# Output projection in block products: a pool per weight tile, later accumulating loads, and all gate sums in one stage

## The chip, the core and the metric

The kernel runs on one core of one Trainium2 chip. The metric is the device time of one execution in microseconds, the median over the runs shown. TensorE (PE) multiplies, VectorE (DVE) and ScalarE (ACT) work on elements, GpSimd (POOL) and SyncE (SP) here mostly issue DMA transfers, each engine from a queue of its own in order.

## The reference

One block of a network over 512 tokens of width 2048, float32 throughout:

```python
sh_a, sc_a, g_a, sh_f, sc_f, g_f = split(silu(c) @ ada_w + ada_b, 6)
h = rms_norm(x, norm_mix) * (1 + sc_a) + sh_a
proj = h @ w_in                       # 2048 x 5656
y_conv = group_norm(short_conv(...))  # 1024 columns, 8 groups of 128
y_attn = head_norm(sparse_attention(...))  # 1024 columns, 8 heads of 128
x = x + g_a * (concat([y_conv, y_attn]) @ w_out)         # 2048 x 2048
h = rms_norm(x, norm_ffn) * (1 + sc_f) + sh_f
x = x + g_f * ((silu(h @ ffn_w1) * (h @ ffn_w3)) @ ffn_w2)   # 2048 x 5632, 5632 x 2048
```

The change touches three places of it: the six conditioning rows (a vector of 2048 times ada_w, 2048 x 12288), the product with w_out, and the place in time at which the row g_f is formed.

## The kernel before

**Arithmetic.** Every large float32 product is three matmuls: each operand is split into a rounded high part and the rest, and high x low, low x high and high x high are added up in PSUM. For a weight tile of 128 x 1024 ACT casts the high part (`whi`) and DVE subtracts it for the low part (`wlo`). Both go to rings of three buffers, so DVE can be about two tiles ahead of PE. An engine runs its queue in order: a DVE instruction that waits for a DMA holds back every `wlo` behind it.

**Stages.** The first fill, norm and the key, value and query columns (to about 320 us); the convolution's columns in eight groups (`conv(c)`), with the attention steps woven in (to 681 us); the output projection (681 to 878); the first projection of the FFN, 44 column blocks (878 to 1749); the second projection (1749 to the end). Within a stage the source gives the order of the work; the framework sets the order of each engine's queue from it by its own planned times, so a transfer or instruction whose wait it expects to end later can fall behind one that stands later in the source. `tc.issue_after(i)` puts what is in its block behind instruction `i` on `i`'s engine.

**Conditioning rows.** They are summed on DVE: for each of 16 slices a piece of ada_w is loaded and added with its factor. `ada(...)` does so with 512 or 1024 columns at once; `gates_beside()` runs steps of it beside the convolutions, at the rates given to `beside`. The gate g_a goes to the DRAM rows `gad[0..3]`. The row g_f (2048 columns in four blocks of 512, 16 sums each) is made by `gate_sums()` (L1739), a generator: each step loads one piece on POOL's queue into `accs` (L1745) and then adds it with the next step (L1748). One buffer holds the piece, so the next load waits for the sum. `next(sums)` stands in the loop of the first projection (every 8th product) and in that of the second (every 3rd unit, L2045).

**Output projection.** The product of the 512 x 2048 input y and w_out is cut into 2 x 2 blocks on both sides, and a Strassen scheme with seven products is used instead of eight: product p (named 2, 1, 5, 6, 3, 7, 4 in this order) multiplies a sum of blocks of y by a sum of blocks of w_out. Each product has eight units (p, j), one for each 128 rows of the weights; a unit is 12 matmuls of 512 columns (4 output tiles x 3 parts, `y_mm`, L1209). The order of the 56 units:

```python
def y_units():
    yield from ((p, j) for p in (2, 1, 5) for j in range(HK))
    for j in range(0, HK, 2):
        yield from ((6, j), (6, j + 1), (3, j), (3, j + 1)) if j in (0, HK - 2) else ((6, j), (3, j), (6, j + 1), (3, j + 1))
    yield from ((p, j) for p in (7, 4) for j in range(HK))
```

`y_load(p, j)` loads the weights of a unit, `y_split` (L1197, L1199) makes `whi` and `wlo` two units ahead, `y_form` (L1040, L1041) splits y's part. The weights of products 1, 5, 6 and 4 share one tile `WT[j]` of a pool `wt` with eight buffers: 1 loads it (L1171), 5 adds another block by an accumulating DMA on POOL (L1173), 6 adds a third on DVE from product 3's tile (L1407), 4 adds a fourth by DMA (L1182). Product 7 loads a tile and accumulates onto it by DMA (L1176 to L1180). The `wt` pool lies where the masks, the attention's keys, values and queries (`qkv`) were, so its loads wait until those are no longer read. The products' sums go through PSUM to `x2T` and others, with x loaded by `x_load` (L1293, L1302) on SP, squared for the next norm, and stored by `x_store` (L1309) on POOL. `at_unit(p, j, ...)` names work ahead of a unit, `behind_unit` work behind it; `yat` gives a unit's number.

The convolution's output is normed late: `norm_y` sums the squares on PE, takes the root on ACT and DVE (L147), stores the row and loads it back to all partitions (L246, L1093, both on POOL), and `scale_y` multiplies (L1100). For the last group this falls into the output projection, and the last sums of y's blocks (`y_sum`, L1028 to L1033) and forms wait for it:

```python
    for n in range(-5, 4):
        if yu[n + 5][0] == 2:
            y_load(*yu[n + 5])
        if n + 2 >= 0:
            y_split(*yu[n + 2])
        if n >= 0:
            y_multiply(*yu[n])

    norm_y()
```

**Second projection.** Again seven products over blocks, in four groups: 154 units of 12 matmuls (L1943; the first unit L1933), with `w_load`, `w_split` (L1529, L1915) and accumulating loads on POOL (L1894, L1899, L1903).

Of the kernel before, what the change touches and what calls it, by code (L numbers as in the profile page):

```python
# [10 lines left out]
F32 = mybir.dt.float32  # L11
F32R = mybir.dt.float32r
# [58 lines left out]
def block_kernel(ctx: ExitStack, tc: tile.TileContext, a: dict, out: bass.AP):  # L71
# [487 lines left out]
    qT = [qp.tile([P, R, S], F32, name=f"qT{g}") for g in range(NKV)]  # L559
# [547 lines left out]
    class Places:  # L1107
# [3 lines left out]
        def tile(self, shape, dtype, tag, name):  # L1111
            self.n += 1
            if shape[1] == 512:
                return kT[self.n % 2][self.n // 2 % 2]
            free = [kTt[:, 0].rearrange("p g s -> p (g s)"), kTt[:, 1].rearrange("p g s -> p (g s)"),
                    yct[:, 6:8, :].rearrange("p c s -> p (c s)")]
            return free[self.n % (3 if self.convs_out < 5 else 2)]
# [3 lines left out]
    def gates_beside():  # L1121
        yield from ffn_part(places, 512, 2)
# [7 lines left out]
        for j in (2, 0):  # L1130
            got = []
            yield from ada(places, 1024, 2 * D + j * 512, 1024, got, bias=True)
            for t in range(2):
                half = got[0][:, t * 512:(t + 1) * 512]
                nc.scalar.activation(half[:, :P], quarters(half), AF.Copy, scale=1.0 if j else -1.0)
                row_of(gad[j + t], half)
            yield
            yield

    later = gates_beside()  # L1140
    weave(beside(convs(), later, (0.3,) * 24 + (0.62,)), attention_steps(), 0.59 / 3)
# [22 lines left out]
    def y_load(p, j):  # L1164
# [3 lines left out]
        elif p == 1:  # L1168
            for q in (1, 5, 6, 4):
                WB[q, j] = in_four(WT[j])  # L1170
            nc.sync.dma_start(WB[p, j], w_block(1, 1, j))  # L1171
        elif p == 5:
# [13 lines left out]
    def y_split(p, j):  # L1186
# [3 lines left out]
        else:  # L1190
            hi, lo = [[wtp.tile([P, 1024], F32R, tag="wt", name="w4")] for _ in range(2)] if p == 4 and j > 4 else \
# [41 lines left out]
    for n in range(-5, 4):  # L1233
        if yu[n + 5][0] == 2:
            y_load(*yu[n + 5])
        if n + 2 >= 0:
            y_split(*yu[n + 2])
        if n >= 0:
            y_multiply(*yu[n])

    norm_y()
# [5 lines left out]
    scale_y()  # L1247
# [17 lines left out]
    wtp = pool("wt", HK, stack=gst)  # L1265
    WT = [wtp.tile([P, 1024], F32, tag="wt", name="wt") for j in range(HK)]
# [22 lines left out]
    def x_load(r, c):  # L1289
        for t in range(2):  # L1290
            if (r, c) == (2, 2):
                for n in range(2):
                    nc.sync.dma_start(x2_of(r, c, t, n),  # L1293
                                      x_of(r, c, t)[:, n * 512:(n + 1) * 512].rearrange("p (a b) -> p a b", a=2))
                continue
# [6 lines left out]
            nc.sync.dma_start(to, x_of(r, c, t).rearrange("p (a b) -> p a b", a=4))  # L1302

# [95 lines left out]

    def at_unit(p, j, *todo):  # L1400
        steps_at.setdefault(yat[p, j], []).extend(todo)

    for j in range(HK):
        at_unit(*yu[4 + j // 2], (y_load, 1, j))
        at_unit(*yu[7 + j], (y_load, 5, j))
# [684 lines left out]
```

## Time and profile before

| | |
|---|---|
| median of 3 runs | 2223.15 us (2222.48 to 2228.21) |
| profiled execution | 2226.84 us, span 2225.1 us |
| granted clock of PE | 0.988 over the span |
| HBM traffic | 428.19 MB read, 19.96 MB written |

A row of groups names line, engine, operation and output <- input. "SPq" and "POOLq" are issues on a DMA queue. A row of waits reads: engine, tile and line, what ended the wait, then total us, how often, and the longest. A row of a timeline: start, duration, engine, line, operation, count, and in brackets the idle time just before it with what ended it. A row of windows: the stretch, its length, then busy us (and count) of PE, PEld (weight load), DVE, ACT and POOL, the granted PE clock, the DMA engines' share and GB/s; for a query of one line the instructions of that line alone. Busy times of pipelined matmuls overlap, so work is better counted in matmuls than in busy time.

### The profile page before, as it was taken

The page shows a single profiled execution, that of the slowest core. Times are in us where ns is not written, and L with a number is a line of the kernel's source. Part 1 is how long each engine was busy: PE and PEld are TensorE (multiplying, and loading weights), DVE is VectorE, ACT ScalarE, POOL GpSimd, SP SyncE. Part 2 cuts the span into 40 slices and gives each one's busy share as a digit, 9 for nine tenths or more (in the row PEclk, how much of TensorE's full clock was granted, in tenths as well). Part 3 has the DMA queues.
Part 4 walks back from the last instruction along what each step waited for, and adds up shares of the span by engine and source line. Part 5 has one row for each costly group of instructions (what it writes and reads, how often), then busy time and mean ns, then how long its engine had stood idle before and what let it go on. Part 6 is the DMA issues. An engine that isn't in the chain of part 4 may idle for free. (4 is left out here: it accounts for less than half of the span.)

```text
span 2225.1 us, 30860 instructions
## 1 busy us (share of the span) xinstructions
PE 2142.4 (96%) x11453; PEld 1789.9 (80%) x11453; DVE 1763.8 (79%) x2574; ACT 1044.1 (47%) x1663; POOL 255.6 (11%) x327
## 2 busy tenths in 40 slices
PE   7999999999998999999999999999999899997999
PEld 6778788887886778888888888888888777886787
DVE  7789568887886776888888878888888677877688
ACT  4235245554454547544444444444444444443343
POOL 0000200000001120001111110111110222212110
PEclk9999999999999999999999999999999999999999
DMA  9976546665665893597777777788685889896775
GB/s 339 364 242 200 181 148 190 190 214 176 211 196 188 220 250 100 147 238 191 191 184 193 188 187 171 186 191 196 176 194 114 281 219 257 231 239 155 241 169 143
DMA packets 449351, 450.19 MB, mean 202 GB/s; under 512 B 20386, under 2 KB 378826, under 8 KB 448560
## 3 DMA queue, kind: packets, MB, share of 16 engines
q1 hardware_dynamic: 376508, 330.90, 47.8%
q0 software_dynamic: 72160, 116.83, 26.4%
q8 instruction: 90, 1.47, 0.3%
q14 instruction: 61, 0.50, 0.1%
q10 hardware_dynamic: 532, 0.48, 0.1%
HBM read 428.19 MB, written 19.96 MB: 201 GB/s over the span
## 5 line engine op out<-in xcount | busy, mean ns | idle before, releaser
L1529 ACT CAST whi<-raw 128x1024 fp32r<-128x1024 f32 x246 | 258.0, 1051 | 260.3 <-PE main L1542 121.9
L1542 PE MATMUL main<-hC,whi 128*128 128x512 f32 x1408 | 346.0, 392 | 1.3 <-DVE d L1561 1.1
L1536 DVE TENSOR_TENSOR wlo<-raw,whi 128x1024 fp32r<-128x1024 f32 x218 | 265.9, 1220 | 100.2 <-PE aux L1548 49.8
L1529 ACT CAST whi<-t 128x1024 fp32r<-128x1024 f32 x186 | 195.4, 1051 | 263.0 <-PE main L1943 69.3
L1542 PEld LDWEIGHTS main<-hC,whi 128*128 128x128 f32 x1408 | 257.4, 188 | 52.6 <-DVE d L1561 2.6
L1542 PE MATMUL aux<-hC,whi 128*128 128x512 f32 x1072 | 264.1, 391 | 0.0
L1542 PEld LDWEIGHTS aux<-hC,whi 128*128 128x128 f32 x1072 | 196.4, 188 | 38.2 <-issue 0.4
L1548 PE MATMUL main<-hC,wlo 128*128 128x256 f32 x1408 | 191.0, 283 | 0.0
L1548 PEld LDWEIGHTS main<-hC,wlo 128*128 128x128 f32 x1408 | 184.8, 191 | 7.7
L121 PE MATMUL main<-alo,whi 128*128 128x512 f32 x432 | 174.6, 404 | 0.0
L122 PE MATMUL main<-ahi,wlo 128*128 128x512 f32 x432 | 170.1, 394 | 0.0
L123 PE MATMUL main<-ahi,whi 128*128 128x512 f32 x432 | 169.9, 394 | 0.0
L1943 PE MATMUL aux<-wlo,ghi 128*128 128x512 f32 x308 | 124.5, 405 | 25.5 <-DVE wlo L1915 25.4
L1548 PE MATMUL aux<-hC,wlo 128*128 128x256 f32 x1072 | 147.6, 283 | 0.0
L1548 PEld LDWEIGHTS aux<-hC,wlo 128*128 128x128 f32 x1072 | 141.7, 191 | 6.1
L1915 DVE TENSOR_TENSOR wlo<-t,whi 128x1024 fp32r<-128x1024 f32 x102 | 123.6, 1219 | 20.4 <-ACT whi L1529 20.1
L1536 DVE TENSOR_TENSOR wlo<-t,whi 128x1024 fp32r<-128x1024 f32 x84 | 102.5, 1220 | 44.5 <-PE aux L1548 21.3
L1519 POOL DMA_DIRECT2D t<-in_ffn_w x42 | 65.0, 1547 | 535.7 <-DVE d L1557 201.9
L1943 PE MATMUL aux<-whi,glo 128*128 128x512 f32 x308 | 123.4, 401 | 0.0
L1943 PE MATMUL main<-wlo,ghi 128*128 128x512 f32 x304 | 120.1, 395 | 3.4 <-DVE wlo L1915 2.8
L1943 PE MATMUL aux<-whi,ghi 128*128 128x512 f32 x308 | 122.7, 398 | 0.0
L1943 PE MATMUL main<-whi,glo 128*128 128x512 f32 x304 | 119.5, 393 | 0.0
(424 smaller groups left out, 4229.2 us busy)
## 6 DMA issues: line engine op xcount, KB each, us to landing
raw<-in_ffn_w SPq DMA_DIRECT2D x204, 512.0 KB, 5.3
t<-in_ffn_w POOLq DMA_DIRECT2D x90, 512.0 KB, 7.2
t<-in_ffn_w SPq DMA_DIRECT2D x78, 512.0 KB, 5.5
kT<-in_ada_w SPq DMA_DIRECT2D x65, 512.0 KB, 4.6
araw<-in_ada_w SPq DMA_DIRECT2D x56, 512.0 KB, 8.7
raw<-in_w_in SPq DMA_DIRECT2D x128, 192.0 KB, 3.7
raw<-in_w_in SPq DMA_DIRECT2D x38, 512.0 KB, 6.8
accs<-in_ada_w POOLq DMA_DIRECT2D x64, 256.0 KB, 3.8
```

What stands on the lines that cost most here:

```text
L121: nc.tensor.matmul(ps, lhs[0], rhs[1], start=first, stop=False)
L122: nc.tensor.matmul(ps, lhs[1], rhs[0], start=False, stop=False)
L123: return nc.tensor.matmul(ps, lhs[0], rhs[0], start=False, stop=last).ins
L1519: nc.gpsimd.dma_start(b["t"].rearrange("p (k n) -> p k n", k=HK), block(u, 12), accum_op=ALU.add)
L1529: hi_ins[-1] = nc.scalar.copy(hi, t).ins
L1536: lo_ins[-1] = nc.vector.tensor_sub(lo, t, hi.bitcast(F32)).ins
L1542: nc.tensor.matmul(ps, wt[0][:, k * P:(k + 1) * P], hc(p, k), start=first and k == 0, stop=False, skip_group_check=True)
L1548: nc.tensor.matmul(ps[:, HS:], wt[1][:, k * P:(k + 1) * P], hc(p, k)[:, 0:HS], start=False, stop=last and k == HK - 1, skip_group_check=True)
L1915: W["last"] = nc.vector.tensor_sub(lo, t, hi.bitcast(F32)).ins
L1943: nc.tensor.matmul(ps[2 * t + c], x_[:, j, tok], w[:, cs], start=m == 0 and j == 0 and p in (1, 5, 2), stop=m == 2 and j == GS[b] - 1 and ...
```

## The change

- The pools: each of the eight `WT[j]` is its own pool of one buffer, and each of the two query tiles `qT` has its own.
- Product 2's loop runs two units further before the rest of the preparation; `norm_y` for the last group stands ahead of it, and `scale_y` behind the last split.
- Product 5's first four weight blocks are loaded plainly on SP into the ring and added on DVE (`w_sum`) instead of accumulated by DMA. Product 1's loads start two units later in the source; product 4's accumulating loads move from units 32 to 39 to units 40 to 45; product 3's first four loads come four units later.
- x's block (2, 2) is loaded in four pieces at units 24 to 30 instead of all at unit 24; x's block (1, 1) two units later; forms, stores and some sums move to other units.
- Beside the convolutions the gate parts come in another order: the FFN part goes last, one g_a part of 1024 columns becomes two of 512, more places serve as buffers, and the rates change.
- `gate_sums` runs in the first projection alone, every 4th product instead of every 8th.

```diff
-    qT = [qp.tile([P, R, S], F32, name=f"qT{g}") for g in range(NKV)]
+    qT = [pool(f"queries{g}", 1, stack=qk).tile([P, R, S], F32, name=f"qT{g}") for g in range(NKV)]
...
-                    yct[:, 6:8, :].rearrange("p c s -> p (c s)")]
-            return free[self.n % (3 if self.convs_out < 5 else 2)]
+                    yct[:, 6:8, :].rearrange("p c s -> p (c s)"), yct[:, 4:6, :].rearrange("p c s -> p (c s)")]
+            n = 4 if self.convs_out < 4 else 3
+            assert self.convs_out < 6
+            return free[self.n % n]
...
     def gates_beside():
-        yield from ffn_part(places, 512, 2)
...
-        for j in (2, 0):
+
+        def gate_out(j, half):
+            nc.scalar.activation(half[:, :P], quarters(half), AF.Copy, scale=1.0 if j > 1 else -1.0)
+            row_of(gad[j], half)
+
+        got = []
+        yield from ada(places, 1024, 2 * D + 1024, 1024, got, bias=True)
+        for t in range(2):
+            gate_out(2 + t, got[0][:, t * 512:(t + 1) * 512])
+        yield
+        yield
+        for j in range(2):
             got = []
-            yield from ada(places, 1024, 2 * D + j * 512, 1024, got, bias=True)
-            for t in range(2):
-                half = got[0][:, t * 512:(t + 1) * 512]
-                nc.scalar.activation(half[:, :P], quarters(half), AF.Copy, scale=1.0 if j else -1.0)
-                row_of(gad[j + t], half)
+            yield from ada(places, 512, 2 * D + j * 512, 512, got, bias=True)
+            gate_out(j, got[0])
             yield
-            yield
+        yield from ffn_part(places, 512, 2)
 
     later = gates_beside()
-    weave(beside(convs(), later, (0.3,) * 24 + (0.62,)), attention_steps(), 0.59 / 3)
+    weave(beside(convs(), later, (0.3,) * 24 + (0.56,) * 120 + (1.08,)), attention_steps(), 0.59 / 3)
...
+        elif p == 5 and j < 4:
+            WB["b", j] = ring_place()
+            nc.sync.dma_start(WB["b", j], w_block(1, 2, j))
         elif p == 5:
             nc.gpsimd.dma_start(WB[p, j], w_block(1, 2, j), accum_op=ALU.add)
...
-            hi, lo = [[wtp.tile([P, 1024], F32R, tag="wt", name="w4")] for _ in range(2)] if p == 4 and j > 4 else \
+            hi, lo = [[wtp[2 * j - 10 + h].tile([P, 1024], F32R, tag="wt", name="w4")] for h in range(2)] if p == 4 and j > 4 else \
...
-    for n in range(-5, 4):
-        if yu[n + 5][0] == 2:
+    norm_y()
+    for n in range(-5, 6):
+        if n + 5 < HK:
             y_load(*yu[n + 5])
         if n + 2 >= 0:
             y_split(*yu[n + 2])
         if n >= 0:
             y_multiply(*yu[n])
 
-    norm_y()
     y_places("H3")
     y_sum("H3", 0, 1)
     for f in ("E5", "H6", "H3"):
         y_sum(f, 2)
     y_form(1, 6)
-    scale_y()
+    with tc.issue_after(low_of[-1]):
+        scale_y()
     y_form(1, 7)
...
-    wtp = pool("wt", HK, stack=gst)
-    WT = [wtp.tile([P, 1024], F32, tag="wt", name="wt") for j in range(HK)]
+    wtp = [pool(f"wt{j}", 1, stack=gst) for j in range(HK)]
+    WT = [wtp[j].tile([P, 1024], F32, tag="wt", name="wt") for j in range(HK)]
...
+    def x22_load(t, n):
+        nc.sync.dma_start(x2_of(2, 2, t, n), x_of(2, 2, t)[:, n * 512:(n + 1) * 512].rearrange("p (a b) -> p a b", a=2))
...
+    def w_sum(to, j, one):
+        nc.vector.tensor_add(WB[to, j], WB[to, j], WB[one, j])
+
     for j in range(HK):
-        at_unit(*yu[4 + j // 2], (y_load, 1, j))
-        at_unit(*yu[7 + j], (y_load, 5, j))
-        at_unit(*yu[(9, 10, 11, 12, 17, 19, 25, 26)[j]], (y_load, 3, j))
-        at_unit(*yu[yat[6, j] - 5], (lambda j: nc.vector.tensor_add(WB[6, j], WB[6, j], WB[3, j]), j))
+        at_unit(*yu[6 + j // 4 if j < 7 else 9], (y_load, 1, j))
+        at_unit(*yu[6 + j if j < 4 else 7 + j], (y_load, 5, j))
+        if j < 4:
+            at_unit(*yu[12 + j], (w_sum, 5, j, "b"))
+        at_unit(*yu[(13, 14, 15, 16, 17, 19, 25, 26)[j]], (y_load, 3, j))
+        at_unit(*yu[yat[6, j] - 4], (lambda j: nc.vector.tensor_add(WB[6, j], WB[6, j], WB[3, j]), j))
         at_unit(*yu[(28, 30, 32, 34, 37, 38, 39, 40)[j]], (y_load, 7, j))
-        at_unit(*yu[32 + j], (y_load, 4, j))
+        at_unit(*yu[(40, 41, 41, 42, 43, 44, 44, 45)[j]], (y_load, 4, j))
...
-    at_unit(1, 0, (x_load, 1, 1))
+    at_unit(1, 2, (x_load, 1, 1))
     at_unit(1, 4, (x_load, 1, 2))
-    at_unit(6, 0, (x_load, 2, 2))
+    for q in range(4):
+        at_unit(*yu[24 + 2 * q], (x22_load, q // 2, q % 2))
...
-    for p, after in ((5, 2), (6, 1), (3, 5), (7, 6), (4, 3)):
-        for j in range(HK):
-            behind_unit(after, j, (y_form, p, j))
+    for j in range(HK):
+        for p, n in ((5, 8 + j), (6, 16 + j), (3, max(23, 22 + j)), (7, 30 + j), (4, 38 + j)):
+            behind_unit(*yu[n], (y_form, p, j))
...
-        behind_unit(*((6, 4), (3, 4), (6, 5), (3, 5))[q], (fifth, t, n))
+        behind_unit(*yu[(30, 32, 33, 35)[q]], (fifth, t, n))
...
-        behind_unit(5, 6, (x_store, 1, 1, t))
-        behind_unit(7, 4, (x_store, 1, 2, t))
+        behind_unit(6, 0, (x_store, 1, 1, t))
+        behind_unit(7, 7, (x_store, 1, 2, t))
...
-    for n in range(4, len(yu)):
-        for what, *args in [t for m in range(4 if n == 4 else 0) for t in behind.pop(m, ())] + steps_at.get(n, []):
+    for n in range(6, len(yu)):
+        for what, *args in [t for m in range(6 if n == 6 else 0) for t in behind.pop(m, ())] + steps_at.get(n, []):
...
-                with tc.issue_after(W.get("last") or lo_ins[-1]):
+                with tc.issue_after(lo_ins[-1]):
                     nc.vector.scalar_tensor_tensor(acc, raw, cT[:, k:k + 1], acc, op0=ALU.mult, op1=ALU.add)
...
-        if n >= SINGLE and n % 8 == 0:
+        if n >= SINGLE and n % 4 == 0:
             next(sums, None)
...
-        if n % 3 == 0 and b < 3:
-            next(sums, None)
         loads(n)
```

More of the change, by code (lines that the diff above doesn't have):

```diff
@@ L1290, in x_load @@
         for t in range(2):
[L1291 to L1295, printed above, removed]
             if r == 2:
@@ L1435, in block_kernel @@
     for jj in range(4):
-        behind_unit(1, 2 + jj, (lambda jj: nc.vector.scalar_tensor_tensor(YF["E5"][jj], YF["H6"][jj], -1.0, YF["H7"][jj],
+        behind_unit(5, 2 * jj, (lambda jj: nc.vector.scalar_tensor_tensor(YF["E5"][jj], YF["H6"][jj], -1.0, YF["H7"][jj],
                                                                      op0=ALU.mult, op1=ALU.subtract), jj))
@@ L1735, in block_kernel @@
             late = new[-1]
-    W = {}
     def gate_sums():
@@ L1839, in block_kernel @@
     y2 = [(yq if t == 3 else yp).tile([P, D], F32, tag="y", name="y") for t in range(NT)]
-    A_, bank = {}, {}
+    W, A_, bank = {}, {}, {}
     def a_parts(b, p):
```

## The prediction

> **What bounds the kernel now.** I read the page first, then busy time by stage, then the waits of TensorE (PE), then the timelines around the longest of them.
>
> ```profile
> PE 2142.4 (96%) x11453; PEld 1789.9 (80%) x11453; DVE 1763.8 (79%) x2574; ACT 1044.1 (47%) x1663; POOL 255.6 (11%) x327
> ...
> core 0: us, PE busy (x) PEld busy (x) DVE busy (x) ACT busy (x) POOL busy (x), PEclk, DMA share, GB/s
> 681.30:878.00 196.70, 172.34 (x765) 139.28 (x764) 137.02 (x193) 101.97 (x182) 34.25 (x45) 0.95 0.74 201
> 878.00:1749.30 871.30, 869.97 (x5009) 765.96 (x5008) 721.09 (x966) 425.33 (x596) 92.19 (x90) 1.00 0.75 183
> 1749.30:2221.00 471.70, 436.80 (x1869) 354.01 (x1867) 366.84 (x372) 203.67 (x198) 98.58 (x140) 0.97 0.81 215
> ...
> 2108.78 16.32 PE main L1943 x72
> ```
>
> PE is the bound, but not evenly. The three stretches are the output projection, the first projection of the FFN and its second projection. The last line, from the chain that ended last, gives the undisturbed pace: 72 matmuls of 512 columns in 16.32 us, 0.2267 us each, 2.72 us for a unit of twelve. The second projection has 154 units, 1848 matmuls: 418.9 us at that pace, and it takes 471.7, so 52.8 us are lost. The first projection loses next to nothing (869.97 busy of 871.30). The output projection:
>
> ```profile
> 681.30:878.00 196.70, 162.81 (x672) 127.96 (x672) 0.95 0.74 201
> 681.30:878.00 196.70, 9.98 (x64) 9.49 (x64) 0.95 0.74 201
> 704.00:747.00 43.00, 29.02 (x113) 21.93 (x114) 26.37 (x41) 19.29 (x34) 8.97 (x12) 0.88 0.93 250
> 812.00:835.00 23.00, 17.80 (x69) 13.61 (x67) 11.40 (x17) 7.59 (x13) 5.50 (x7) 0.93 1.08 258
> ```
>
> The first two lines are the products (L1209) and the turning of the result (L1369) alone. 672 x 0.2267 is 152.3; with 9.98 and about 2 for other transposes 164.3 are needed, so 32.4 us are lost. In 704 to 747 only 113 matmuls ran: 43 - 25.6 = 17.4 lost. In 812 to 835, 69 ran: 23 - 15.6 = 7.4 lost. What PE waited for:
>
> ```profile
> PE aux L1943 <- DVE wlo L1915: 25.4, 9, 4.5
> PE aux L1209 <- DVE wlo L1199: 20.5, 10, 10.7
> PE aux L241 <- DVE accs L1748: 4.8, 1, 4.8
> ```
>
> Both large waits are for the low part of a weight tile (wlo), which VectorE (DVE) makes. The question is why DVE was late.
>
> **Part 1: all gate sums in the first projection.** Of 64 sums (L1748), 32 run in the second projection today:
>
> ```profile
> L1748 DVE SCALAR_TENSOR_TENSOR accs<-accs,cT x30: 743/750/754, 1777.9 to 2076.1; 128x512 f32<-128x512 f32 x30
>   DMA accs<-in_ada_w: 44.5, 15
> 1777.95 0.75 DVE L1748 SCALAR_TENSOR_TENSOR accs<-accs,cT 128x512 f32<-128x512 f32 x1 [7.41 <-DMA accs<-in_ada_w]
> 1779.89 0.79 PE L1943 MATMUL aux<-wlo,ghi 128*128 128x512 f32 x1 [4.51 <-DVE wlo L1915]
> 2029.31 0.80 PE L1943 MATMUL main<-wlo,ghi 128*128 128x512 f32 x1 [2.62 <-DVE wlo L1915]
> ```
>
> The first line is the sums after 1766 us, the second what ended DVE's idle time before them. A sum at the head of DVE's queue waits 7.41 us for its load, the next wlo stands behind it, and PE idles 4.51 us; PE then restarts slowly (0.79 us against the usual 0.39). Each PE wait of over 1 us in this stage has such a sum just ahead of it. So PE's wait (25.4 + 4.8, and 2.8 on the other bank set) is the sums' doing, and so is most of the lost clock (0.97 over 471.7 us, some 14 us): 47 of the 52.8.
>
> The change takes out 32 sums, 32 loads, and two quarter-sums with their stores. What is late next? At the stage's start the DMA engines are full:
>
> ```profile
> 1750.00:1800.00 50.00, 40.51 (x168) 32.00 (x166) 31.38 (x32) 20.70 (x23) 10.20 (x14) 0.97 1.02 290
> 2150.00:2200.00 50.00, 50.00 (x223) 41.39 (x222) 45.92 (x52) 24.52 (x23) 7.00 (x9) 1.00 0.72 171
> ```
>
> Weights might be late there once PE runs through. The last line, without sums, loses nothing, so this concerns the start alone, where 54 matmuls of the 222 are missing (12.2 us). I let 7.8 of the 52.8 stay and take 45; the ends are 37 (all the start's loss comes back, and a few small waits) and 52.8.
>
> The price in the first projection: the generator has 68 steps and is now called 70 times there instead of 35, every 4 products. It adds 32 sums.
>
> ```profile
> L1748 DVE SCALAR_TENSOR_TENSOR accs<-accs,cT x32: 736/741/744, 995.2 to 1710.0; 128x512 f32<-128x512 f32 x32
>   POOL accs L1745: 207.6, 28
> DMA to landing us min/median/max: 2.9/3.7/8.6
> 1106.60 0.74 DVE L1748 SCALAR_TENSOR_TENSOR accs<-accs,cT 128x512 f32<-128x512 f32 x1
> 1128.87 0.74 DVE L1748 SCALAR_TENSOR_TENSOR accs<-accs,cT 128x512 f32<-128x512 f32 x1
> ```
>
> 32 x 0.74 is 23.7 us on a DVE idle for 871.3 - 721.1 = 150.2 us of the stage. None of these sums waited for its load: the load waited for the sum (207.6 us on POOL). Eight products take 22.3 us, four 11.1; issue (about 1) and the slowest landing (8.6) still fit. The accumulating `t` loads share POOL's queue; one standing behind an accs load that waits for its sum is held up by a product or two, of the six it has in hand. I take 1 us, between 0 and 23.7 (were all sums on the path): nearest to the row without a DMA wait.
>
> **Part 2: weight tiles of the output projection, earlier.**
>
> ```profile
> 707.13 0.38 SPq L1302 DMA_DIRECT2D x2T<-in_x  x1
> 707.56 5.30 SPq L1171 DMA_DIRECT2D wt<-in_w_out  x8
> SPq L1302 <- DVE H L1033: 7.6, 1, 7.6
> 703.71 0.75 DVE L1100 SCALAR_TENSOR_TENSOR yc<-yc,cols,cc 128x512 f32<-128x512 f32 x1 [5.55 <-DMA cc<-rsd]
> 714.66 0.77 PE L1209 MATMUL aux<-wlo,form 128*128 128x512 f32 x1 [10.69 <-DVE wlo L1199]
> 729.15 0.50 PE L1209 MATMUL aux<-wlo,form 128*128 128x512 f32 x1 [0.82 <-DVE wlo L1199]
> ```
>
> Product 2 ends at 704. The eight `wt` loads of product 1 issue at 707.56, all together, behind an x load in SP's queue that waited 7.6 us for the last sum over the convolution output; that sum waited for the last norm (scale_y at 703.71, itself 5.55 us after its row's load). PE idles 10.69 us and then runs a unit each 3.75 us, with waits like that at 729.15, because the loads arrive so. In the change each tile is its own pool and need wait only for what lay in its own place, mostly done by 687; x loads come two units later, so the loads can go out behind product 2's last (689). Norm_y a few units earlier brings scale_y some 6 us forward, and issue_after puts it behind the last split, so no wlo stands behind its wait. For product 5 four plain SP loads and four additions (1.23 us each by the row of the next such addition, below: 4.9 us on a DVE idle 16.6 of these 43 us) replace four POOL loads. Bytes: 43 us x 250 GB/s is 10.7 MB; starting at 689 instead of 707 moves 18 us of it under product 2. I keep 2 of the 17.4: gain 15.4, ends -5 (loads as late as today, additions on the path) and 17.4.
>
> ```profile
> 741.96 1.23 DVE L1407 TENSOR_TENSOR wt<-wt,raw 128x1024 f32<-128x1024 f32 x1
> POOL wt L1182 <- DVE wlo L1199: 20.0, 5, 9.4
> 820.12 1.04 ACT L1197 CAST whi<-x2T 128x1024 fp32r<-128x1024 f32 x1 [6.81 <-DMA x2T<-in_w_out]
> 822.47 0.50 PE L1209 MATMUL aux<-wlo,form 128*128 128x512 f32 x1 [3.02 <-DVE wlo L1199]
> 837.31 0.46 PE L1369 MATMUL main<-dg,x2T 128*128 128x128 f32 x2 [2.46 <-issue]
> ```
>
> Product 4's accumulating loads (L1182) wait on POOL for splits of product 6 (20.0 us), and product 7's loads queue behind them: 7's tiles land late, ACT waits 6.81 us, PE 3.02 at 822 and 2.02 at 827, and the norm behind ACT's late casts costs 2.46 at 837. Issued at units 40 to 45, product 4's loads no longer stand ahead; they keep six units (16.3 us) to land. Product 7's own chain of load, then accumulating load, stays tight, so of 7.4 + 3.7 I keep 3.5: gain 7.6, ends 0 and 11. Moving the forms, x22 loads, and stores costs nothing: DVE and ACT idle for 59.7 and 94.7 us here, and SP's x22 loads are spread to the units where their place comes free. With a rest of 1 the stage gains 24.
>
> **Part 3: conv stage.** One 1024-wide gate part becomes two 512-wide ones: 32 x 0.74 instead of 16 x 1.28 (rates of the rows for such sums), 3 us more on DVE, and an FFN part moves to the end. PE has few gaps there. I take 1, between 0 and 4.
>
> ```profile
> 656.88 1.28 DVE L219 SCALAR_TENSOR_TENSOR accs<-kT,cT,accs 128x1024 f32<-128x1024 f32 x1 [0.97 <-DMA kT<-in_ada_w]
> ```
>
> Sum: 45 + 24 - 1 - 1 = 67. The profiled execution took 2226.8 (span 2225.1 and 1.7 around it): 2159.8. The median shown, 2223.15, is 3.7 lower, so 2156.
>
> [...] The clock, by rows: its shortfall is 14 us in the second projection and 5 in 704 to 747 (0.12 x 43), 19 in all. [...]
>
> [...] The shares of 0.93 and 1.08 above say that the DMA engines were nearly full where PE waited (rival B). [...]
>
> **Rivals.** A: the `wt` loads still go out late (another wait in SP's queue replaces the x load's). For it: SP is in order, and the framework set the x load ahead of loads written earlier. Part 2 then gains 8.6 instead of 24: 2171. B: DMA capacity replaces the waits: product 1 and 5, product 7 and the start of the second projection stay fed at 250 to 290 GB/s. For it: shares near 1; against it: without sums 8 MB (32 x 256 KB) leave the second projection, and the loads start 18 us sooner. Half of 17.4, all of 11 and all of 12.2 stay: 24 - 16 = 8 and 37, so 2223 - 43 = 2180. C, the other side: the sums stall DVE in the first projection as they did in the second. There 32 cost about 47 us, 1.5 each; if all 64 cost that, 94, the kernel gains 45 + 24 - 94 - 1 = -26: 2249. It passes no change at 68/64 = 1.1 us per sum, that is from landings of some 13 us on. Against it: 8.6 at most in that stage. [...] D: it changes nothing; the waits come from DVE being full. Against it: DVE idles right before the late sums. 2223.
>
> **How the numbers follow.** Forecast case 0.56 (2146 to 2167: part 1 between 37 and 52.8, the rest within 3), A 0.14, B 0.14, E 0.08, C 0.04, D 0.04. The range reaches from 2144 to 2186 and so takes in A and B. About 0.3% (7 us) is what a measurement can tell from no change. Faster 0.93, same 0.03, slower 0.04.
>
> **What would show it.** Right: no L1748 after 1700 us, PE near 60 matmuls of 512 columns in each 13.6 us of the second projection, `wt` loads issued before 695, no PE gap at product 1, scale_y near 698, product 7 without a wait over 1 us. Wrong: DVE sums in the first projection ended by their DMA; an SP wait ahead of the `wt` loads; PE waits ended by weight DMA at the start of the second projection.

## The result, and the profile after

The changed kernel takes 2151.99 us (median of 4 runs, 2150.01 to 2152.95) against 2222.82 us for the kernel before in the same session: ratio 0.9676, 95% interval 0.9658 to 0.9695. The forecast was 2156, range 2144 to 2186. The profiled execution took 2152.95 us with a span of 2151.2, 73.9 less than before, at a granted clock of 0.998 (before 0.988).

The page's first lines, then the same three stages in windows (columns as in the section on the profile before), then two stretches around the opening of product 1, and the opening of the second projection:

```profile
span 2151.2 us, 30977 instructions
PE 2121.4 (99%) x11453; PEld 1781.6 (83%) x11453; DVE 1770.0 (82%) x2594; ACT 1045.0 (49%) x1665; POOL 252.6 (12%) x324
...
675.70:851.20 175.50, 166.78 (x764) 138.07 (x762) 140.16 (x195) 101.51 (x181) 30.88 (x41) 0.97 0.77 208
851.20:1724.50 873.30, 872.77 (x5026) 766.17 (x5025) 742.37 (x998) 425.32 (x599) 111.80 (x124) 1.00 0.78 191
1724.50:2147.00 422.50, 420.50 (x1853) 346.94 (x1852) 346.18 (x340) 202.76 (x196) 79.30 (x106) 1.00 0.85 222
...
676.00:704.00 28.00, 28.00 (x130) 22.78 (x129) 23.77 (x31) 15.95 (x27) 3.28 (x6) 1.00 0.71 230
704.00:747.00 43.00, 43.00 (x191) 35.61 (x191) 43.00 (x60) 25.93 (x44) 8.20 (x10) 1.00 0.82 217
1750.00:1800.00 50.00, 50.00 (x222) 41.39 (x222) 37.98 (x36) 28.27 (x33) 14.89 (x22) 1.00 1.03 295
```

| stage | before | after | difference | forecast |
|---|---|---|---|---|
| to the end of the convolutions | 681.3 | 675.7 | -5.6 | +1 |
| output projection | 196.7 | 175.5 | -21.2 | -24 |
| first projection | 871.3 | 873.3 | +2.0 | +1 |
| second projection | 471.7 | 422.5 | -49.2 | -45 |

The same instructions of PE run (11453); what went is time between them, and slow matmuls behind the waits (0.79 us for the first one at 1779.89 before). In 704 to 747 us 191 matmuls ran in place of 113, at a granted clock of 1.00 (before 0.88). At the opening of the second projection, with the DMA engines at a share of 1.03 (before 1.02), PE now runs through: 222 matmuls in 50 us where there were 168.

The waits of PE that are left after 675 us, the gate sums, the loads of product 1 and the last norm's scaling (all of the kernel after; a source row gives count, shortest/median/longest ns, first and last start):

```profile
PE main L1380 <- issue: 4.5, 1, 4.5
PE aux L1221 <- DVE wlo L1211: 4.3, 2, 3.6
...
PE main L1959 <- DVE wlo L1931: 1.0, 1, 1.0
...
L1764 DVE SCALAR_TENSOR_TENSOR accs<-accs,cT x64: 740/744/745, 958.1 to 1697.6; 128x512 f32<-128x512 f32 x64
  POOL accs L1761: 332.1, 45
DMA to landing us min/median/max: 2.9/4.7/8.0
L1180 SPq DMA_DIRECT2D wt<-in_w_out x8: 328/423/1767, 661.3 to 697.2; - x8
692.43 0.74 DVE L1100 SCALAR_TENSOR_TENSOR yc<-yc,cols,cc 128x512 f32<-128x512 f32 x1
```

The last of the 64 sums starts at 1697.6, and none waited for its load: the loads (POOL, L1761) waited for the sums, 332.1 us in all. Product 1's tiles are loaded from 661 to 697 us instead of together at 707.56, and the last norm is applied at 692.43 instead of 703.71. What stays is product 7:

```profile
797.26 0.80 PE L1221 MATMUL aux<-wlo,form 128*128 128x512 f32 x1 [3.65 <-DVE wlo L1211]
802.22 0.50 PE L1221 MATMUL aux<-wlo,form 128*128 128x512 f32 x1 [0.62 <-DVE wlo L1211]
812.45 3.90 PE L1380 MATMUL main<-dg,x2T 128*128 128x128 f32 x16 [4.45 <-issue]
...
767.99 1.17 POOL L1194 DMA_DIRECT2D wt<-in_w_out  x1
778.46 1.31 POOL L1192 DMA_DIRECT2D x2T<-in_w_out  x1 [9.29 <-issue]
779.21 1.46 POOL L1194 DMA_DIRECT2D wt<-in_w_out  x1
...
794.90 1.04 ACT L1209 CAST whi<-x2T 128x1024 fp32r<-128x1024 f32 x1 [6.46 <-DMA x2T<-in_w_out]
808.09 1.14 ACT L1209 CAST w<-raw 128x512 fp32r<-128x512 f32 x2 [4.07 <-DMA raw<-in_w_out]
```

POOL's queue still alternates between product 7's accumulating loads (L1192) and product 4's (L1194), although the source now places product 4's six to eight units later. From 739 to 795 us the sixteen loads go out for the products 4, 4, 4, 4, 7, 4, 7, 4, 7, 4, 7, 4, 7, 7, 7, 7, which is the order of the kernel before (from 765 to 821 us there): the framework set it, and the move in the source didn't change it. The tile `x2T` lands at 794.90 and PE idles 3.65 us.

### The profile page after: what moved, and what is told of

It reads as the page before. It is cut to its first block, busy times and chain, and to the rows that moved or that the text cites. A ratio compares the mean times of both kernels' runs of the same rounds, so it can differ in the third digit from the quotient of the medians.

```text
span 2151.2 us, 30977 instructions
## 1 busy us (share of the span) xinstructions
PE 2121.4 (99%) x11453; PEld 1781.6 (83%) x11453; DVE 1770.0 (82%) x2594; ACT 1045.0 (49%) x1665; POOL 252.6 (12%) x324
## 4 chain that ended last, share of the span: by engine, by line
PE 91%; DMA 4%; DVE 3%; issue 1%; ACT 1%; POOL 0%; SPq 0%; DVEq 0%; ACTq 0%; POOLq 0%
PE main L1560 15%; PE aux L1560 11%; PE aux L1959 9%; PE main L1959 9%; PE main L1566 8%; PE aux L1566 6%; PE main L121 5%; PE main L122 5%; PE main L123 5%; PE aux L1221 3%; PE main L1221 2%; PE aux L121 2%; PE aux L123 2%; PE aux L122 2%; PE aux L986 2%; DMA raw<-in_w_out 1%
## 5 line engine op out<-in xcount | busy, mean ns | idle before, releaser
L121 PE MATMUL main<-alo,whi 128*128 128x512 f32 x432 | 173.6, 402 | 0.0
L1959 PE MATMUL aux<-wlo,ghi 128*128 128x512 f32 x308 | 119.7, 389 | 0.0
L1959 PE MATMUL main<-whi,ghi 128*128 128x512 f32 x304 | 118.3, 389 | 0.0
```

The costliest lines, as they stand in the source:

```text
L121: nc.tensor.matmul(ps, lhs[0], rhs[1], start=first, stop=False)
L1959: nc.tensor.matmul(ps[2 * t + c], x_[:, j, tok], w[:, cs], start=m == 0 and j == 0 and p in (1, 5, 2), stop=m == 2 and j == GS[b] - 1 and ...
```

## The experiments

Twelve kernels. Ratios are to the kernel before, measured in the same session; stage lengths are from one profiled execution each. The five kernels whose output projection has all its edits and no other (the kernel after, and below out_only, sums_2, sums_3 and sums_twice) took 175.5, 173.0, 174.4, 173.1 and 173.6 us there, so a stage that differs from the 175.5 by 2 us shows nothing by that alone.

### 1. The three parts one at a time

Each is the kernel before with one group of the edits (the diff stands in the section on the change): the gate sums; the edits beside the convolutions; the output projection with its pools.

sums_only:

> The kernel before with the gate sums alone moved (called every 4th product of the first projection, not at all in the second). Theory of the held queue (a gate sum that waits for its load at the head of DVE's queue holds back the low parts behind it): second projection 471.7 -> 422 to 424 us, first projection 871.3 -> 873 (as in the changed kernel), the rest as before: 2222.8 - 47.5 = 2175. Rival, capacity (the second projection gained because fewer bytes and DVE instructions ran there): the same direction, but then the 32 sums moved cost a like amount in the first projection, which runs at 0.75 DMA share and 83% DVE: 871.3 -> 885 or more, total above 2187. Rival, interaction (part of the 49 us came from the output projection ending sooner): second projection above 435, total above 2187.

conv_only:

> The kernel before with the order, widths and rates of the gate parts beside the convolutions alone changed. Theory: the 5.6 us by which the convolution stage ended sooner in the changed kernel come from this edit, since it takes away the PE wait of 3.2 us at 519 us and its slow restart: the stage ends at 675.5 to 676.5 instead of 681.3 and the kernel takes 2217 to 2218. Rival (the forecast's): the edit costs 1 us, and the 5.6 came from the split query pools: the stage ends at 681 to 682, total 2223 to 2224.

out_only:

> The kernel before with all edits of the output projection alone (pools, loads, norm, forms, stores). Theory: the three parts add up, so the output projection takes 175.5 us instead of 196.7 and the kernel 2201 to 2203; the wait at the first unit of product 1 is gone, those of product 7 stay. Rival, interaction (the earlier free buffers of the new order beside the convolutions are needed for the early wt loads): the wait at product 1 partly returns, the stage takes 180 us or more, total 2206 or more.

| kernel | median us | ratio, 95% interval | conv. end | output proj. | first | second |
|---|---|---|---|---|---|---|
| sums_only | 2175.15 | 0.9786 (0.9768 to 0.9803) | 680.1 | 194.0 | 873.3 | 420.8 |
| conv_only | 2223.45 | 0.9997 (0.9985 to 1.0008) | 680.4 | 196.2 | 872.0 | 470.6 |
| out_only | 2203.36 | 0.9915 (0.9892 to 0.9939) | 677.4 | 173.0 | 872.5 | 471.8 |

Measured against 2223.42, the sums bring 48.3, the output projection 20.1 and the convolutions nothing: 68.4 together, of the 71 between the medians of the kernels before and after (by the ratios 66 of 72). The second projection of the kernel with the sums alone, and PE's waits in it:

```profile
1747.40:2168.20 420.80, 419.97 (x1851) 346.55 (x1849) 345.62 (x340) 202.87 (x196) 79.34 (x106) 1.00 0.85 223
PE main L1931 <- DVE glo L1867: 0.5, 1, 0.5
```

Without the sums the waits and the lost clock (1.00 granted in this stage, 0.97 before) are gone together, so both were theirs. The theory of a gain beside the convolutions fell: the wait at 519 us (3.23) is gone there, yet the kernel takes the same time. In out_only, with the gate order of before, the wait is still there and the convolutions end at 677.4: its granted clock from 500 to 560 us was 1.00, in the kernel before 0.97, which is 1.8 of the 3.9 us between the two. That wait, and a matmul about a microsecond behind it, in the kernel before and then in out_only:

```profile
519.31 0.66 PE L1004 MATMUL aux<-const,o 128*128 128x128 f32 x4 [3.23 <-DVE sc L908]
520.60 0.63 PE L121 MATMUL main<-alo,whi 128*128 128x512 f32 x1
```
```profile
517.68 0.66 PE L1004 MATMUL aux<-const,o 128*128 128x128 f32 x4 [3.04 <-DVE sc L908]
518.87 0.40 PE L121 MATMUL main<-alo,whi 128*128 128x512 f32 x1
```

Behind the wait of 3.23 us the matmuls took 0.63 us each from 520.60 to 523.16; behind that of 3.04 us they took 0.39 to 0.40 from 518.41 on. In profiled executions the convolutions ended at 681.3, 680.1 and 677.4 us with the old gate order, and between 675.7 and 680.4 in eleven with the new one (mean 677.4 against 679.6): two microseconds, less than the executions differ among themselves. The same fourteen part cleanly by another edit: 680.1 to 681.3 us in the three kernels without the edits of the output projection (before, sums_only, conv_only), 675.7 to 678.3 in the eleven with them, means of 680.6 and 677.2. So some 3 us of the shorter start go with those edits, among them the split query pools that conv_only's rival named; which of them does it, and how, no run shows.

### 2. One pool for all weight tiles

```diff
-    wtp = [pool(f"wt{j}", 1, stack=gst) for j in range(HK)]
-    WT = [wtp[j].tile([P, 1024], F32, tag="wt", name="wt") for j in range(HK)]
+    wtp = pool("wt", HK, stack=gst)
+    WT = [wtp.tile([P, 1024], F32, tag="wt", name="wt") for j in range(HK)]
```

> The changed kernel with the eight wt tiles in one pool of eight buffers again; source order, norm and all else as changed. Theory of the held queue: what freed the first loads is that each tile waits for its own place alone; with one pool they fall behind the first x load again, which waits for the last sum over the convolution output (about 695 us now that the norm is sooner), so the first wt tile lands near 700 and PE waits 3 to 6 us at product 1, with some smaller waits and clock behind it: +4 to +9 us, 2156 to 2161. Rival 1 (source order and the sooner norm did it, the pools nothing): 2152, wt loads before 695. Rival 2 (it was bytes: four accumulating loads fewer): 2152 as well, with the loads late but no wait.

2164.36 us, ratio 0.9738 (0.9717 to 0.9758), output projection 185.5 us: 12.4 us slower than the kernel after, more than expected. On its timeline the loads go out in one piece, right behind the first x load (L1310), which waits for the last sum over the convolution output (H) and so for the last norm (L1100), and the first of them is missed at 704.90; then the windows up to 747 us:

```profile
693.78 0.74 DVE L1100 SCALAR_TENSOR_TENSOR yc<-yc,cols,cc 128x512 f32<-128x512 f32 x1
SPq L1310 <- DVE H L1033: 2.8, 1, 2.8
697.26 0.38 SPq L1310 DMA_DIRECT2D x2T<-in_x  x1
697.69 4.57 SPq L1180 DMA_DIRECT2D wt<-in_w_out  x8
704.90 0.80 PE L1221 MATMUL aux<-wlo,form 128*128 128x512 f32 x1 [5.22 <-DVE wlo L1211]
677.00:704.00 27.00, 22.68 (x107) 18.04 (x105) 21.62 (x34) 13.47 (x22) 3.29 (x6) 0.96 0.62 203
704.00:747.00 43.00, 41.96 (x176) 34.24 (x177) 37.48 (x47) 23.46 (x38) 6.43 (x8) 0.95 0.90 281
```

That is what the theory expected: in SP's queue all eight loads stand behind product 5's plain loads and that x load, as they stood behind an x load in the kernel before. With a pool for each tile seven of the eight stand ahead of it, the first at 661, and only the last goes out behind it, at 697. Why the framework puts the loads of one pool so late no run shows; a release of the pool as a whole in its plan would explain it. In the 70 us to 747 PE issues 283 matmuls here; the kernel after issues 321 from 676 to 747, or 317 in 70 us. The 34 missing ones are 7.7 us at 0.2267; the other 4.7 us come later (the wait at product 7 is 5.37 us here). Even so this kernel's loads leave 9.9 us sooner than before (707.56), and its last norm is applied 9.9 us sooner (693.78 instead of 703.71): with one pool the loads follow the norm, so the rest of the gain at the opening goes with the sooner norm there.

### 3. Norm late, and product 5 accumulated again

norm_late is the kernel after with `norm_y()` behind the first loop; b_accum with product 5's first four blocks accumulated through POOL instead of loaded plainly and added on DVE:

```diff
-        elif p == 5 and j < 4:
-            WB["b", j] = ring_place()
-            nc.sync.dma_start(WB["b", j], w_block(1, 2, j))
...
-        at_unit(*yu[6 + j if j < 4 else 7 + j], (y_load, 5, j))
-        if j < 4:
-            at_unit(*yu[12 + j], (w_sum, 5, j, "b"))
+        at_unit(*yu[7 + j], (y_load, 5, j))
```

> The kernel after, with the last norm behind the first loop of the output projection again, as before. Held-queue theory: product 1 opens when its weights land, not when the norm comes; the norm's scale moves from 692 us to about 706 us, product 1's seventh block needs it near 716 us: nothing to 3 us lost, 2152 to 2155 us. Rival: the norm on its own opened the stage, and its chain of two small transfers again stands between product 2 and product 1: a gap of 8 to 13 us near 700 us, 2160 to 2165 us.

> The kernel after, with product 5's first four blocks accumulated through POOL again (eight accumulating loads in place of four; the four plain loads and the four VectorE sums are gone). Held-queue theory: these loads go behind product 1's splits of the same tiles, 9 to 12 us from issue to landing, and product 5 begins near 722 us: the first block lands late by 0 to 3 us, 2152 to 2155 us. Rival: the accumulating loads are what held product 5 before, and a gap of 5 us or more opens at product 5: 2157 us or more. Rival with the other sign: without four sums of VectorE (1.1 us each) the stage is shorter by 1 to 3 us: 2149 to 2151 us.

norm_late: 2157.32 us, ratio 0.9696 (0.9679 to 0.9714). b_accum: 2155.17, ratio 0.9688 (0.9671 to 0.9706). Both intervals overlap that of the kernel after, so by time they aren't told from it, though the fastest execution of each (2154.10 and 2153.42) is slower than the slowest of the kernel after (2152.95, in another session). The stretch of products 1 and 5, and the wait at product 7, first of norm_late, then of b_accum:

```profile
704.00:747.00 43.00, 42.61 (x188) 34.80 (x188) 40.85 (x61) 29.78 (x57) 10.15 (x14) 1.00 0.80 217
800.97 0.80 PE L1221 MATMUL aux<-wlo,form 128*128 128x512 f32 x1 [5.31 <-DVE wlo L1211]
```
```profile
704.00:747.00 43.00, 43.00 (x192) 35.59 (x191) 39.35 (x54) 25.68 (x44) 9.86 (x12) 1.00 0.93 225
801.88 0.79 PE L1218 MATMUL aux<-wlo,form 128*128 128x512 f32 x1 [4.76 <-DVE wlo L1208]
```

With either edit undone PE is fed in 704 to 747 us. While the pools are separate, neither the earlier norm nor the plain loads is needed to open product 1 and 5: in norm_late the norm is applied at 703.10 us, and seven of the eight `wt` loads still leave from 662 to 675. Both undone at once was not tried. The output projection takes 177 us in either, and the wait at product 7 is 5.31 and 4.76 us, where the longest one of the five kernels named above is 1.8 to 3.7; so the two edits may bring some 2 us there, which these runs don't settle.

### 4. How fast may the gate sums come?

The forecast's rival on the other side (C) was that the sums stall DVE in the first projection. sums_2 and sums_3 space them by two and three products instead of four. sums_twice keeps four and gives DVE a second instruction of the same shape between two sums, which needs no load:

```diff
-        if n >= SINGLE and n % 4 == 0:
+        if n >= SINGLE and n % 2 == 0:      # sums_2; n % 3 in sums_3
```
```diff
-            next(sums, None)
+            under_way = next(sums, None)
+        elif n >= SINGLE and n % 4 == 2 and under_way:
+            acc = accs[:, 1, :]
+            with tc.issue_after(lo_ins[-1]):
+                nc.vector.scalar_tensor_tensor(acc, acc, 0.0, acc, op0=ALU.mult, op1=ALU.add)
```

sums_2:

> The kernel after, with a gate sum every second product of the first projection in place of every fourth (one every 5.6 us instead of 11.2 us, so that they end near 1330 us). It tests the point from which the forecast's rival of sums that stall VectorE decides: a load takes about 5 us from issue to landing, and the next one waits for the sum. Theory: 64 sums at 0.744 us cost what they cost now, and VectorE waits little for a load: 2151 to 2156 us. Rival: at this spacing VectorE, which works in order, stands at each sum for its load, 1 to 2 us each, and TensorE runs dry behind it: 2165 us or more.

2221.03 us (median of 12), ratio 0.9988 (0.9976 to 1.0): 69 us slower than the kernel after, the whole gain of the change. The theory fell, and the rival was right. Its waits on DVE, and the stretch with the sums:

```profile
DVE accs L1764 <- DMA accs<-in_ada_w: 81.4, 33, 8.5
950.00:1390.00 440.00, 387.64 (x2132) 331.88 (x2130) 337.33 (x459) 173.16 (x248) 68.02 (x87) 0.96 0.76 185
```

33 of the 64 sums stood at the head of DVE's queue until their load landed. PE was busy for 88% of these 440 us at a clock of 0.96. DVE was busy for only 77%; was it the wait for loads, or the denser work?

sums_3:

> The kernel after, with a gate sum every third product of the first projection (8.4 us apart; 11.2 us after, 5.6 us in the kernel with one every second product, which took 2221 us). Theory of the load wait: one turn of the single buffer is issue 0.55 us, landing 2.9 to 8.0 us with 4.7 us in the middle, sum 0.74 us, so 4.2 to 9.3 us; at 8.4 us only the longest few stand in VectorE: first projection 873 to 882 us, 2152 to 2161 us. Rival, VectorE's share of work: the loss goes with the rate of sums, a third of the way from 2152 to 2221 us: about 2175 us.

sums_twice:

> The kernel after, with a second VectorE instruction of the same shape halfway between two gate sums (acc times zero plus acc, which changes no value) and no further load: VectorE has as many of these per us as with a sum every second product, but half the loads. Theory of the load wait: it was the wait of VectorE for the load that cost 69 us; some 62 further instructions at 0.744 us are 46 us of VectorE's work beside TensorE's, 0 to 10 us lost: 2152 to 2162 us. Rival, VectorE's capacity: 2200 us or more, TensorE at 90% while the sums run.

sums_3: 2151.58 us (2145.55 to 2158.95), ratio 0.9664 (0.9640 to 0.9688); sums_twice: 2151.82, ratio 0.9665 (0.9649 to 0.9681). Neither is told from the kernel after. The added instructions of sums_twice and its stretch with the sums; then the wait of sums_3:

```profile
L1806 DVE SCALAR_TENSOR_TENSOR accs<-accs x64: 677/681/685, 952.2 to 1692.4; 128x512 f32<-128x512 f32 x64
950.00:1700.00 750.00, 749.97 (x4309) 657.43 (x4308) 678.44 (x931) 352.90 (x499) 98.99 (x107) 1.00 0.80 193
```
```profile
DVE accs L1764 <- DMA accs<-in_ada_w: 15.0, 9, 3.4
```

In sums_twice DVE was busy for 90% (678.44 of 750) and PE for 749.97, so the 69 us of sums_2 are no matter of DVE's capacity. The loss came where the turn of the one buffer (issue, landing, sum) no longer fitted between two places: no sum waits at 11.2 us, nine wait at 8.4 (in the slowest of the four executions, whose first projection took 881 us), half of them at 5.6. That the single buffer is the cause, rather than the loads as such, was not tried with a second buffer.

### 5. What holds product 7

hold_p4 puts product 4's accumulating loads behind product 7's in POOL's queue (in its trace one of them still goes ahead of product 7's last). norm_first puts the norm of the upper half, which the 16 small matmuls at 812.45 need, ahead of product 7's last two splits on ACT. hold_norm has both.

```diff
-            nc.gpsimd.dma_start(WB[p, j], w_block(2, 2, j), accum_op=ALU.add)
+            seven[-1] = nc.gpsimd.dma_start(WB[p, j], w_block(2, 2, j), accum_op=ALU.add).ins
         elif p == 4:
-            nc.gpsimd.dma_start(WB[p, j], w_block(2, 1, j), accum_op=ALU.add)
+            with tc.issue_after(seven[-1]):      # product 7's last accumulating load so far
+                nc.gpsimd.dma_start(WB[p, j], w_block(2, 1, j), accum_op=ALU.add)
```
```diff
-    behind_unit(7, 4, (norm_of, 0, dg0[:, 0]), (norm_of, 1, dg0[:, 1]))
+    behind_unit(7, 3, (norm_of, 0, dg0[:, 0]), (norm_of, 1, dg0[:, 1]))
...
+        with tc.issue_after(rooted[1]) if p == 7 and j > 5 else ExitStack():      # the norm's last square root on ACT
             for h, r in zip(hi, at):
                 nc.scalar.copy(h.rearrange("p (a b) -> p a b", a=w), src[:, r])
```

hold_p4:

> The kernel after, with product 4's accumulating loads ordered behind product 7's last one on POOL's queue (in the kernel after, three of product 4's stand between product 7's, at 768.0, 779.2 and 780.6 us). Held-queue theory: product 7's fourth block then lands some 4 us sooner, the PE gap of 3.65 us at 797.3 us and the 0.62 us at 802.2 us go, product 4's blocks land by 820 us and are in time; the output projection takes 171 us instead of 175.5, the time is 2146 to 2149 us. Capacity rival: the accumulating queue is simply full between 755 and 810 us, so what product 7 gains product 4 loses: a gap of 2 to 5 us at product 4's blocks, 2151 to 2156 us. Second rival: the plain load that goes before product 7's accumulation (issued at 764.5 and 768.7 us, landed near 778 us) sets the time alone, the gap stays at 797 us, 2152 us.

2150.49 us, ratio 0.9666 (0.9648 to 0.9685): not told from the kernel after. The gaps at 797 and 802 us are gone as expected, but the next one grew from 4.45 to 7.57 us. The stage takes 173.1 us, which is within the 173.0 to 175.5 of the five kernels without this edit, and not the 171 expected:

```profile
811.30 3.90 PE L1382 MATMUL main<-dg,x2T 128*128 128x128 f32 x16 [7.57 <-issue]
806.93 1.14 ACT L1211 CAST w<-raw 128x512 fp32r<-128x512 f32 x2 [8.19 <-DMA raw<-in_w_out]
```

ACT stands at a split that waits 8.19 us for its load, and the norm's last square stands behind it. That is what norm_first takes away:

> The kernel after, with the norm of the finished upper half ahead of product 7's last two splits on ScalarE's queue (norm_of one unit sooner, the two splits ordered behind its square roots). Theory, ScalarE held at a wait for a load: TensorE's wait of 4.45 us at 812.5 us is for that norm, whose last square and roots stand behind the split that waits 4.07 us for its load; with the norm first, the 16 small matmuls (3.90 us) fill that wait: output projection 171 to 172.5 us instead of 175.2, 2147 to 2150 us. Rival, the last block's landing near 808 us sets the time: the gap moves behind the small matmuls to product 7's last two blocks, 174 to 175 us, 2151 to 2152 us.

> Both edits on the kernel after: product 4's accumulating loads behind product 7's, and the norm ahead of product 7's last two splits. Theory: the two waits go together, since the first edit alone only moved its gain into the wait for the norm (3.65 and 0.62 us gone at product 7, 4.45 grown to 7.57 us): the last block is split near 809 us, product 7 ends some 6 us sooner than with the first edit alone, output projection 167 to 169 us, 2144 to 2147 us. Rival: product 4's blocks, of which one landed at 821.4 us with the first edit alone, are late next: a gap of 2 to 5 us there, 170 to 172 us, 2147 to 2150 us.

norm_first: **2145.60 us** (2145.15 to 2146.70), ratio 0.9636 (0.9621 to 0.9652), whose interval lies below that of the kernel after: the best version. hold_norm: 2149.69 us, ratio 0.9653 (0.9638 to 0.9669). The output projection of norm_first, its remaining gap, the norm's roots on ACT and the small matmuls; then hold_norm's stage and its gap:

```profile
676.40:844.20 167.80, 164.36 (x763) 136.11 (x762) 140.19 (x195) 101.37 (x181) 30.77 (x41) 0.99 0.80 218
800.78 0.50 PE L1223 MATMUL aux<-wlo,form 128*128 128x512 f32 x1 [3.11 <-DVE wlo L1213]
804.66 0.61 ACT L146 ACTIVATE r<-r,eps_t 128x1 f32<-128x1 f32 x2
807.99 1.95 PE L1382 MATMUL main<-dg,x2T 128*128 128x128 f32 x16
```
```profile
677.20:846.20 169.00, 164.70 (x764) 136.10 (x763) 140.56 (x195) 101.06 (x181) 30.83 (x41) 0.99 0.80 217
823.95 0.80 PE L1225 MATMUL aux<-wlo,form 128*128 128x512 f32 x1 [2.94 <-DVE wlo L1215]
819.42 1.05 ACT L1213 CAST w<-wt 128x1024 fp32r<-128x1024 f32 x1 [7.78 <-DMA wt<-in_w_out]
```

The norm is ready before PE reaches the small matmuls, which run in 1.95 us instead of 3.90, with no wait just ahead of them: 4.45 + 1.95 are 6.4 us, and the medians differ by 6.4 (the profiled stages by 7.7, with the stage of the kernel after the longest of the five). The theory named the place and undersized it, as it left the clock out (granted from 785 to 845 us: 0.91 in the kernel after, 0.97 here). With both edits product 4's tile is late (7.78 us on ACT, 2.94 on PE): the rival's gap, though the stage itself is 169.0 us as the theory had it. The first projection takes 876.5 us there, 3 more than after; its first loads now follow product 4's, which would explain it, but that was not tried.

## Why the prediction was right, step by step

**Second projection, 45 foreseen, 49.2 measured.** The mechanism held, and sums_only shows it by itself. The size was off in one step: 7.8 us were kept back for weights that would be late at the opening. They were not: 222 matmuls in 1750 to 1800 us with the DMA engines at 1.03. Rival B is refuted there: at that share PE was busy for all of the 50 us.

**First projection, +1 foreseen, +2.0 measured.** Three kernels without the added sums took 871.3 to 872.5 us in this stage, the kernel after and sums_only 873.3. Rival C does not occur at the change's spacing, but it is real: at half of it all is lost. The forecast put its turning point at 1.1 us per sum; sums_2 lost 69 / 64 = 1.08 and ended at 2221.03, next to 2223.65. It said from landings of some 13 us on, at 11.2 us between sums. With the sums 5.6 us apart a median landing of 3.8 us was enough.

**Opening of product 1, 15.4 foreseen, all 17.4 came back.** Loads out from 661, no gap, scale_y at 692 (foreseen near 698). The cause was named but not weighed: the prediction added up pools, later x loads, norm and plain loads. The later place of the x loads in the source didn't do it by itself: with one pool the `wt` loads stand behind an x load again, which costs 7.7 us here. The norm and the plain loads, undone one at a time, cost nothing here while the pools are separate; with one pool the loads follow the norm. Whether the pools alone, put into the kernel before, bring all 17.4 was not tried. Rival A needed a wait in SP's queue ahead of the loads; with one pool there is such a wait, for the sum H behind the norm, and the kernel takes 2164 (the rival: 2171). One row was misread: scale_y at 703.71 is not 5.55 us after its row's load; DVE stood idle 5.55 us until that load landed. No term hangs on it.

**Product 7, 7.6 foreseen, little or nothing came.** This is the step that failed: "Issued at units 40 to 45, product 4's loads no longer stand ahead". In POOL's queue the order of the two products' loads is that of before, four of product 4's among product 7's. PE's waits there are 8.7 us in all (4.3 + 4.5, rounded), against 3.02 + 2.02 + 2.46 and 1.24 more for the norm, 8.7 as well, before; in out_only, sums_2, sums_3 and sums_twice they are 6.4 to 7.9. And the order in the queue was not the only binding step: hold_p4 got it right and neither its time nor its stage shows a gain, because the norm behind ACT's split was next. Norm_first regains 6.4 us by its median (7.7 by the profiled stage), about what was foreseen, by another edit.

By matmuls the stage lost 32.4 us before and loses 175.5 - 164.3 = 11.2 now: 21.2 regained, of which 17.4 at the opening, none at product 7, and some 4 in the rest, where 1 was foreseen; what brought those 4 stays open. That 24 came near is partly luck: the opening and the rest were 5 too small, product 7 was 7.6 too large.

**Convolutions, +1 foreseen, -5.6 in the profile.** The edit alone changes nothing that can be measured (0.9985 to 1.0008). Some 3 of the 5.6 go with the edits of the output projection (mean end 677.2 against 680.6), an effect that the prediction didn't have and whose cause stays open; the rest is within what single executions differ by.

**Rival E** (0.08), that 9 us of the lost clock stay, is refuted. Those 9 us were the author's estimate, and no run shows them. What the runs showed in their place: the granted clock is 0.998 over the span (before 0.988), and 1.00 in the second projection of sums_only, where the sums' waits are gone (before 0.97). The lost clock went with the waits, also with one of 2.62 us (2029.31 in the kernel before, 0.80 us for the first matmul behind it).

The forecast is 4 us above the measured 2152: the terms miss by 4 at the second projection and 6.6 at the start one way, by 2.8 and 1 at the others the other way, which makes the 7 by which the spans of the two profiled executions differ from the forecast (73.9 against 67); the medians differ by 71. Rival B's 2180 is some 5 us too high by its own terms: with half of 17.4, all of product 7's loss and all of 12.2 staying, 24 becomes 9.7 and 45 becomes 40.6, which gives 2175.

## What to carry to other kernels

In hold_p4 ACT stood 8.19 us at a split whose load was late, and PE waited 7.57 us for the norm behind it: look at what is behind each late load rather than at the load. Moving the short chain (a norm, a root) ahead of it gained 6.4 us (norm_first); putting product 4's loads behind product 7's gained nothing that can be told (hold_p4). Spread loads through one buffer so that issue, landing and use fit between two uses: here sums 8.4 us apart cost nothing that can be told (2151.58), sums 5.6 us apart cost 69 us. A place in the source is not a place in a queue (product 4's loads, six to eight units later in the source, kept their order on POOL): read the queue's order from the trace before a move is priced.

## What the runs showed of the hardware

- Between 950 and 1700 us in sums_twice DVE was 90% busy (678.44 of 750 us) and PE 749.97 us; between 950 and 1390 in sums_2, with waits for loads in it, DVE was 77% busy and PE lost 12% (387.64 of 440).
- In these runs the length of the wait just ahead didn't tell whether the matmuls of 512 columns behind it took 0.39 us or 0.63. The first one took 0.80 and the next ones 0.63 after 2.62 us (before, at 2029.31) and 2.94 (hold_norm, at 823.95). After 3.20 (sums_only, at 519.24) and 3.23 (before, at 519.31) they took 0.63 too, in the latter from 520.60 on; after 3.04 (out_only, at 517.68) 0.39 to 0.40 from 518.41 on. After 3.11 in norm_first (at 800.78) the first took 0.50, and 0.63 came from 801.72 to 804.28.
- With the DMA engines at a share of 1.03 and 295 GB/s PE was busy for all of 1750 to 1800 us in the kernel after (222 matmuls).
